# Past rows of the convolutions stored in one piece per partition, evictions of the in-projection ranked first, and 32x32 products alternating between two quadrants

## The chip, the cores and the metric

The kernel runs on one core of a Trainium2 chip. The metric is the device time of one execution in microseconds (us), from three runs. A profile of one further execution gives the spans and rows used below; its TensorE clock is told as the granted clock, 1.00 for 2.4 GHz and 0.50 for 1.2 GHz.

## The reference, cut to what matters

One inference step of a decoder trunk of two layers, all in float32, for a prompt of 512 tokens without a past and 8 samples of one token each with a past. Layer 0 mixes tokens by causal pooling, layer 1 by a gated delta rule over 8 heads of 128; each is followed by a ConvFFN. The three convolutions need the last rows of the past, and the new past rows are outputs.

```python
def conv_ffn(xn, buf, w_up, conv_w, conv_b, w_down):       # buf: last 2 up-projected rows
    hh = jnp.concatenate([buf, xn @ w_up], axis=1)
    c = causal_depthwise_conv(hh, conv_w, t) + conv_b      # width 3
    gate, val = jnp.split(c, 2, axis=-1)
    return (jax.nn.silu(gate) * val) @ w_down, hh[:, -2:]

def deltanet_mixer(xn, conv_buf, s0, w_in, conv_w, ...):   # conv_buf: last 3 rows
    qkv, z, a, bb = jnp.split(xn @ w_in, ...)              # 1024 -> 4096 + 16
    qkv_all = jnp.concatenate([conv_buf, qkv], axis=1)
    q, k, v = jnp.split(silu(causal_depthwise_conv(qkv_all, conv_w, t)), 3)   # width 4
    o, s_new = gated_delta_rule(l2_norm(q) * 128 ** -0.5, l2_norm(k), v, g, beta, s0)
    o = rms_norm(o, o_norm_w) * silu(z)
    return o @ w_out, qkv_all[:, -3:], s_new               # rows and state are outputs
```

The delta rule is computed in chunks: a unit lower triangular matrix per chunk and head is inverted, and a scan over the chunks carries a 128x128 state S.

## The kernel before

**Layout.** Everything lies with channels on the 128 partitions and the 520 columns (512 of the prompt, 8 of the samples) along the free axis, in two halves of 256 and 264 columns. A weight matrix comes in chunks of 128x1024 (`wr`), by DMA from the SP queue two chunks ahead; ACT casts each to the upper part `wh`, DVE subtracts to get the lower part `wl`, and each product is three TensorE matmuls (`ps<-xh,wl`, `ps<-xl,wh`, `ps<-xh,wh`).

**The delta layer.** Its in-projection has 32 tiles (`tile_`, from line 1619): two halves of 24 matmuls each, into a ring of three PSUM half-banks, so that a half can begin when the one three before it has been evicted. The task `t_post` (line 1559) evicts both halves on DVE (`hb<-ps,rstd`, two `hb` buffers), then does the convolution: one ACT and three DVE operations (`c<-hb,vec,c`), SiLU on ACT. Beside the tiles run, for each of four pairs of heads: `t_em` and `t_head` (decay factors `em`, which come back spread over the partitions by the DMA `em<-gdr`, and the matrix `U`), `t_leaf` and `levels` (inversion: `levels` at line 1285 joins blocks of 32 to 64 to 128 by small products; the tiles `p1` and `p2` take 32x32 products, both named `p` in the trace), `t_scan` (the chain over four chunks: `p_s` on PE, `rho` on DVE, `ut` on ACT, `S` on DVE), `t_norm` (output `ot`, transposed into `pt`, times the gate into `oz`), and `t_sample`, the single step of the eight samples for this pair (state loads `s<-in_ssm`, one for each head, products `p_q`, small DVE operations `s_...`, result `so`). `t_split` makes `oh` and `ol`, the two parts of the out-projection's input, for one head each.

**The end of the layer.** After the last in-projection tile, line 1667 on, SP stores the new past rows (`dnc_p`, `dnc_s`) and then loads the first two residual tiles `x<-xsp`. The out-projection starts on the heads that are ready (k = 0 to 5, for two of its eight output tiles), and goes on to the heads of the last pair when their `oh` and `ol` are there. Its eviction adds `x`.

**What sets the order.** The program is written out at build time. `Clock` models when each engine is free; `Background` (line 252) holds tasks sorted by a priority number (lower goes first). Between matmuls `step` lets the first task go on whose operands, engine and condition are ready in the model. `t_post` has priority 1, waits until the model sees DVE free (`"DVE"` as second part of its `yield`), and has `t_em` at 1, `t_scan` at 0.8, `t_head` at 0.6 and `t_leaf` at 0.5 beside or ahead of it; `t_sample` has 3.5.

**The FFN.** 44 tiles of two halves per layer in the up-projection. For each, the past rows enter the sample columns, and POOL copies the last rows of `hb` into the buffers of the outputs (`st<-hb`, 8 columns, and `fo<-hb`, 2 columns). One load at the start and two stores at the end of the up-projection move them.

All instructions carry line 152 in the trace, the helper that records them, so rows are told apart by tiles.

Of the kernel before, what the change touches and what calls it, by code (L numbers as in the profile page):

```python
# [14 lines left out]
T, B = 512, 8  # L15
NT = T + B
# [371 lines left out]
def _emit(tc, nc, clk, E, P, a, o):  # L388
    V, S, G, PE, SP = (E[k] for k in ("DVE", "ACT", "POOL", "PE", "SP"))
# [32 lines left out]
    bc = lambda v, shape, axis: v.unsqueeze(axis).broadcast_to(shape)  # L422
# [35 lines left out]
    bg = Background(clk)  # L458
# [138 lines left out]
    def ffn_buffers(p):  # L597
        return p.tile([128, NE, 3, B], F32, "st")

    fcw = lambda l, i: vec[:, V_FC + (l * 3 + i) * NE:V_FC + (l * 3 + i) * NE + NE]  # L600

    def ffn_load(l, buf):
        SP.dma_start(out=buf[:, :, 0:2, :], in_=a["ffn_buf"][l])

# [200 lines left out]
    def ffn(l, res, buf, mk, half0):  # L805
        rstd = res.rstd
        with scope(f"ff{l}") as fp:
            gh = fp.tile([128, KF, NT], F32R, "gh")
            gl = fp.tile([128, KF, NT], F32R, "gl")
            fo = fp.tile([128, NE, 2], F32, "fo")  # L810
            if buf is None:
                buf = ffn_buffers(fp)
                ffn_load(l, buf)
            st = buf
# [10 lines left out]
            for e in range(NE):  # L825
# [4 lines left out]
                hb = hbuf()  # L830
# [13 lines left out]
                for i in (1, 0):  # L844
                    V.scalar_tensor_tensor(
                        out=c[:, T:], in0=st[:, e, i, :], scalar=cw(i)[:, e:e + 1], in1=c[:, T:], op0=ALU.mult, op1=ALU.add
                    )
                G.tensor_copy(st[:, e, 2, :], hb[:, 3 + T:])
                G.tensor_copy(fo[:, e, :], hb[:, 1 + T:3 + T])
                if e % 2 == 0:  # L850
# [7 lines left out]
            finish(pend)  # L858
            SP.dma_start(out=o["ffn_p"][l], in_=fo)
            SP.dma_start(out=o["ffn_s"][l], in_=st[:, :, 1:3, :])  # L860
            nr = mk()
# [98 lines left out]
    def delta_in(res, dp, oz, oz1, r8):  # L960
# [19 lines left out]
        for v in vts:  # L980
            G.memset(v, 0.0)
        dst = dp.tile([128, 24, 3, B], F32, "dst")
        SP.dma_start(out=dst, in_=a["dn_buf"])
        dsb = dp.tile([128, 24, B], F32, "dsb")
        dtm = dp.tile([128, 24, B], F32, "dtm", tag="lx")
        cw = lambda i: vec[:, V_DC + i * 24:V_DC + i * 24 + 24]
        G.tensor_tensor(out=dsb, in0=dst[:, :, 0, :], in1=bc(cw(0), [128, 24, B], 2), op=ALU.mult)
        for i in (1, 2):
            G.tensor_tensor(out=dtm, in0=dst[:, :, i, :], in1=bc(cw(i), [128, 24, B], 2), op=ALU.mult)
            G.tensor_tensor(out=dsb, in0=dsb, in1=dtm, op=ALU.add)  # L990
# [298 lines left out]
        def levels(hh, vc, wc):  # L1289
# [14 lines left out]
            t0 = clk.at["PE"]  # L1304
            for i in (0, 2):
                s0, s1 = slice(32 * i, 32 * i + 32), slice(32 * i + 32, 32 * i + 64)
                for q in range(N2):
                    PE.matmul(p1[s1, q * 32:q * 32 + 32], u(q)[s0, s1], wc[s0, q, :], start=True, stop=True)
# [7 lines left out]
            p2 = aux("p2")  # L1316
            t0 = clk.at["PE"]
            s1 = slice(32, 64)
            for q in range(N2):
                PE.matmul(p2[s1, q * 32:q * 32 + 32], vc[s1, q, :], ysb[s1, q, :], start=True, stop=True)  # L1320
            for i in (0, 2):
                s0, s1 = slice(32 * i, 32 * i + 32), slice(32 * i + 32, 32 * i + 64)
                for q in range(N2):
                    PE.matmul(p2[s0, q * 32:q * 32 + 32], ysb[s1, q, :], vc[s1, q, :], start=True, stop=True)
            lite(t0)
# [232 lines left out]

        def t_post(i, n, halves, dst_ap, fin, pre):
            yield [halves[0], rstd[:]], "DVE", lambda: (i < 2 or i - 2 in read) and (i < 3 or i - 3 in posted)  # L1560
            hb = hbuf()
            for j in range(2):
                if j:
                    yield [lambda: clk.ready(halves[1]) + 0.1], "DVE", lambda: i in emitted
                V.tensor_tensor(out=hb[:, 3 + HS[j].start:3 + HS[j].stop], in0=halves[j], in1=rstd[:, HS[j]], op=ALU.mult)
                half_read.add((i, j))
            yield [hb[:]], "ACT", pre
            dst_ap = dst_ap() if callable(dst_ap) else dst_ap
# [46 lines left out]
        def tile_(n, dst_ap, fin, pre=None):  # L1615
            i = idx[0]
            idx[0] += 1
            bg.until(lambda: W.nl > W.nt and (i < 2 or (i - 2, 1) in half_read))
            ring = ((2 * i - 2) % 3, (2 * i - 1) % 3) if i else (2, 3)
            bg.settle(max([psd["p"].free_at(f"r{ring[0]}", 1)] + [clk.ready(w[:]) for w in W.peek()]) + 0.27)  # L1620
            halves = [dense_half(ring[0], 0), None]

            def mid():
                bg.add(t_post(i, n, halves, dst_ap, fin, pre), 1)
                bg.until(lambda: i < 1 or (i - 1, 0) in half_read)
                bg.settle(psd["p"].free_at(f"r{ring[1]}", 1) + 0.27)
# [39 lines left out]
        bg.until(lambda: n_in - 1 in posted and n_in - 2 in posted)  # L1666
        SP.dma_start(out=o["dnc_p"], in_=dnew[:, :, 0:3])
        SP.dma_start(out=o["dnc_s"][:, :, 0:2, :], in_=dst[:, :, 1:3, :])
        SP.dma_start(out=o["dnc_s"][:, :, 2, :], in_=dnew[:, :, 3:])
        for n, parts in (("oh", oh), ("ol", ol)):  # L1670
# [50 lines left out]
_OUT = {  # L1721
    "y": (128, KD, NT), "pool_p": (15, D), "pool_s": (128, KD, B, 15), "dnc_p": (128, 24, 3), "dnc_s": (128, 24, 3, B),
    "dns_p": (NH, 128, 128), "dns_s": (B, NH, 128, 128), "ffn_p": (2, 128, NE, 2), "ffn_s": (2, 128, NE, 2, B),
}


def _pack(i):
# [25 lines left out]
        "dn_out": c(tiles(i["dn_w_out"][0], KD).reshape(KD, 128, KD * 128)),  # L1753
        "ffn_buf": c(i["state_ffn_conv"].reshape(2, B, 2, NE, 128).transpose(0, 4, 3, 2, 1)[:, :, order]),
        "dn_buf": c(i["state_dn_conv"][0].reshape(B, 3, 24, 128).transpose(3, 2, 1, 0)),
        "ssm": c(i["state_dn_ssm"][0]),
# [34 lines left out]
```

## Time and profile before

| | |
|---|---|
| three runs | 1178.58, 1173.41, 1178.0 us; median 1178.0 |
| profiled execution | 1176.59 us, span 1174.9 us, mean granted clock 0.992 |
| PE | busy 1143.4 us, 97% of the span, 9576 matmuls |
| DVE | busy 793.5 us, 68% |
| ACT | busy 518.2 us, 44% |
| POOL | busy 404.6 us, 34% |
| chain that ended last | PE 87%, DVE 5%, DMA 3%, SP's queue 2% |

PE is the engine that is nearly always busy; what the others do matters where PE waits. In the table of stretches a stretch in which PE is busy 12.50 of 12.50 us has no wait to take away. A row of a timeline that ends in brackets tells how long the engine was idle before it and what ended that. The delta layer lies between about 425 and 755 us.

### The profile page before, as it was taken

To read this page: it belongs to the slowest core of one execution; us is meant where nothing else is said; L and a number is where in the kernel's file an instruction comes from. 1 tells how busy PE (TensorE), PEld (TensorE's weight loads), DVE (VectorE), ACT (ScalarE), POOL (GpSimd) and SP (SyncE) were. 2 spreads that over 40 slices of the span, in tenths; PEclk is the share of its full clock that TensorE was granted. 3 is DMA by queue.
4 is the path that set the end of the run, shared out by engine and by line. 5 is a ranking of instruction groups with operands and counts; after the bars stand their busy time and mean duration, and the time that the engine had idled before them with its cause. 6 is when DMAs were issued, how large, how long until landed. Compare 5 with 4: busy or idle time off the path is not lost.

```text
span 1174.9 us, 23548 instructions
## 1 busy us (share of the span) xinstructions
PE 1143.4 (97%) x9576; PEld 1120.8 (95%) x9576; DVE 793.5 (68%) x1464; ACT 518.2 (44%) x959; POOL 404.6 (34%) x610
## 2 busy tenths in 40 slices
PE   9999999999999999999899999799999999999996
PEld 8999999999999998999799998799999999999996
DVE  7877777777333377866778765469998989952224
ACT  5544444444322247765566734444444444432222
POOL 4233222222000011555463360225555555511011
PEclk9999999999999999999999999999999999999998
DMA  9222232323433233332233239535445444552322
GB/s 285 92 90 91 90 93 90 102 90 95 128 108 103 92 124 91 102 99 62 71 96 100 68 109 27 153 87 170 144 139 149 145 126 144 148 134 85 98 81 73
DMA packets 100974, 128.45 MB, mean 109 GB/s; under 512 B 37276, under 2 KB 72860, under 8 KB 100867
## 3 DMA queue, kind: packets, MB, share of 16 engines
q1 hardware_dynamic: 100723, 126.69, 38.8%
q8 instruction: 75, 1.23, 0.4%
q10 hardware_dynamic: 144, 0.26, 0.1%
q14 instruction: 32, 0.26, 0.1%
HBM read 116.20 MB, written 10.74 MB: 108 GB/s over the span
## 4 chain that ended last, share of the span: by engine, by line
PE 87%; DVE 5%; DMA 3%; SPq 2%; ACT 1%; issue 1%; DVEq 0%; POOL 0%; ACTq 0%; POOLq 0%
PE ps L152 78%; PE ps_d L152 2%; SPq L152 2%; DMA em<-gdr 1%; PE p L152 1%; PE p_s L152 1%; PE pk L152 1%; PE p_q L152 1%; DVE wl L152 1%; PE pt L152 1%; DVE em L152 1%; DVE c L152 1%; PE po L152 1%; DVE x L152 1%; DMA s<-in_ssm 1%
## 5 line engine op out<-in xcount | busy, mean ns | idle before, releaser
L152 PE MATMUL ps<-xh,wl 128*128 128x264 f32 (+1 forms) x1920 | 547.4, 285 | 6.1 <-DVE hb L152 6.1
L152 PE MATMUL ps<-xl,wh 128*128 128x256 f32 (+2 forms) x1936 | 550.5, 285 | 0.0
L152 PE MATMUL ps<-xh,wh 128*128 128x256 f32 (+2 forms) x1936 | 550.0, 284 | 0.0
L152 PEld LDWEIGHTS ps<-xh,wl 128*128 128x128 f32 x1920 | 362.4, 189 | 9.4 <-DVE hb L152 7.1
L152 PEld LDWEIGHTS ps<-xh,wh 128*128 128x128 f32 (+1 forms) x1936 | 364.1, 188 | 1.3 <-issue 0.8
L152 PEld LDWEIGHTS ps<-xl,wh 128*128 128x128 f32 (+1 forms) x1936 | 363.8, 188 | 1.5 <-issue 0.8
L152 DVE TENSOR_TENSOR wl<-wr,wh 128x1024 fp32r<-128x1024 f32 (+1 forms) x175 | 217.3, 1242 | 107.9 <-ACT wh L152 107.9
L152 ACT CAST wh<-wr 128x1024 fp32r<-128x1024 f32 (+1 forms) x177 | 180.4, 1020 | 215.8 <-PE ps L152 174.3
L152 DVE SCALAR_TENSOR_TENSOR c<-hb,vec,c 128x512 f32<-128x512 f32 x248 | 219.2, 884 | 11.1 <-ACT c L152 6.7
L152 POOL COPY st<-hb 128x8 f32<-128x8 f32 x88 | 73.0, 830 | 301.4 <-DVE hb L152 301.4
L152 PE MATMUL ps<-gl,wh 128*128 128x256 f32 (+1 forms) x616 | 174.5, 283 | 0.0
L152 PE MATMUL ps<-gh,wl 128*128 128x256 f32 (+1 forms) x616 | 174.0, 283 | 0.0
L152 PE MATMUL ps<-gh,wh 128*128 128x256 f32 (+1 forms) x616 | 173.8, 282 | 0.0
L152 DVE TENSOR_TENSOR hb<-ps,rstd 128x520 f32<-128x520 f32 (+2 forms) x152 | 87.5, 581 | 88.6 <-PE ps L152 87.9
L152 ACT ACTIVATE c<-hb,vec 128x520 f32<-128x520 f32 x112 | 89.9, 804 | 87.9 <-DVE hb L152 86.9
L152 POOL TENSOR_TENSOR acc<-acc,sq 128x520 f32<-128x520 f32 (+2 forms) x30 | 40.7, 1356 | 243.0 <-ACT sq L152 243.0
L152 PEld LDWEIGHTS ps<-gh,wh 128*128 128x128 f32 x616 | 116.3, 189 | 0.0
L152 PEld LDWEIGHTS ps<-gl,wh 128*128 128x128 f32 x616 | 115.9, 188 | 0.0
L152 PEld LDWEIGHTS ps<-gh,wl 128*128 128x128 f32 x616 | 115.7, 188 | 0.0
L152 ACT CAST gh<-c 128x520 fp32r<-128x520 f32 x44 | 27.6, 628 | 109.6 <-DVE c L152 109.6
L152 POOL COPY fo<-hb 128x2 f32<-128x2 f32 x88 | 74.2, 843 | 0.0
L152 ACT ACTIVATE sg<-c 128x520 f32<-128x520 f32 x44 | 28.1, 639 | 94.4 <-DVE c L152 94.4
(273 smaller groups left out, 1403.4 us busy)
## 6 DMA issues: line engine op xcount, KB each, us to landing
wr<-in_up SPq DMA_DIRECT2D x88, 512.0 KB, 3.5
wr<-in_dn_in SPq DMA_DIRECT2D x32, 512.0 KB, 3.5
wr<-in_down SPq DMA_DIRECT2D x32, 448.0 KB, 3.3
wr<-in_down SPq DMA_DIRECT2D x16, 512.0 KB, 3.5
s<-in_ssm SPq DMA_DIRECT2D x8, 512.0 KB, 4.1
wr<-in_dn_out SPq DMA_DIRECT2D x8, 512.0 KB, 3.5
s<-in_ssm SPq DMA_DIRECT2D x16, 256.0 KB, 4.0
s_ub<-udr SPq DMA_DIRECT2D x16, 256.0 KB, 4.4
```

The lines of the kernel that those rows point to most:

```text
L152: r = f(*a, **k)
```

## The change

Three edits, independent of each other.

1. The buffers of past rows are turned round, `[partition, channel tile, row, sample]` to `[partition, row, channel tile, sample]`, and the new row goes with the prompt's rows (`dnew`, `fo`), so that each load and store is one contiguous piece per partition; the outputs are put together on the host. For the FFN, one POOL copy of 10 columns takes the place of two of 8 and 2.
2. The eviction of an in-projection tile becomes a task of its own, `t_evict`, with priority -1, and no longer asks that the model see DVE free. `t_post` follows with the rest.
3. The 32x32 products of `p1` and two thirds of those of `p2` are issued alternately for two pairs of quadrants of the PE array; before, one quadrant's came after the other's.

```diff
-        return p.tile([128, NE, 3, B], F32, "st")
+        return p.tile([128, 2, NE, B], F32, "st")
-        SP.dma_start(out=buf[:, :, 0:2, :], in_=a["ffn_buf"][l])
+        SP.dma_start(out=buf, in_=a["ffn_buf"][l])
...
-                G.tensor_copy(st[:, e, 2, :], hb[:, 3 + T:])
-                G.tensor_copy(fo[:, e, :], hb[:, 1 + T:3 + T])
+                G.tensor_copy(fo[:, e, :], hb[:, 1 + T:])
...
-            SP.dma_start(out=o["ffn_p"][l], in_=fo)
-            SP.dma_start(out=o["ffn_s"][l], in_=st[:, :, 1:3, :])
+            SP.dma_start(out=o["ffn_n"][l], in_=fo)
+            SP.dma_start(out=o["ffn_o"][l], in_=st[:, 1])
...
-        dst = dp.tile([128, 24, 3, B], F32, "dst")
+        dst = dp.tile([128, 3, 24, B], F32, "dst")
...
-            for i in (0, 2):
-                s0, s1 = slice(32 * i, 32 * i + 32), slice(32 * i + 32, 32 * i + 64)
-                for q in range(N2):
+            for q in range(N2):
+                for i in (0, 2):
+                    s0, s1 = slice(32 * i, 32 * i + 32), slice(32 * i + 32, 32 * i + 64)
                     PE.matmul(p1[s1, q * 32:q * 32 + 32], u(q)[s0, s1], wc[s0, q, :], start=True, stop=True)
...
             for q in range(N2):
                 PE.matmul(p2[s1, q * 32:q * 32 + 32], vc[s1, q, :], ysb[s1, q, :], start=True, stop=True)
-            for i in (0, 2):
-                ...
-                    PE.matmul(p2[s0, q * 32:q * 32 + 32], ysb[s1, q, :], vc[s1, q, :], start=True, stop=True)
+                second(2, q)
+            for q in range(N2):
+                second(0, q)
...
-        def t_post(i, n, halves, dst_ap, fin, pre):
-            yield [halves[0], rstd[:]], "DVE", lambda: (i < 2 or i - 2 in read) and (i < 3 or i - 3 in posted)
+        def t_evict(i, n, halves, dst_ap, fin, pre):
+            yield [lambda: clk.ready(halves[0]) + 0.1, rstd[:]], None, lambda: (i < 2 or i - 2 in read) and (i < 3 or i - 3 in posted)
             hb = hbuf()
             for j in range(2):
                 if j:
-                    yield [lambda: clk.ready(halves[1]) + 0.1], "DVE", lambda: i in emitted
+                    yield [lambda: clk.ready(halves[1]) + 0.1], None, lambda: i in emitted
                 V.tensor_tensor(out=hb[:, 3 + HS[j].start:3 + HS[j].stop], in0=halves[j], in1=rstd[:, HS[j]], op=ALU.mult)
                 half_read.add((i, j))
+            bg.add(t_post(i, n, hb, dst_ap, fin, pre), 1)
...
-                bg.add(t_post(i, n, halves, dst_ap, fin, pre), 1)
+                bg.add(t_evict(i, n, halves, dst_ap, fin, pre), -1)
...
-        SP.dma_start(out=o["dnc_p"], in_=dnew[:, :, 0:3])
-        SP.dma_start(out=o["dnc_s"][:, :, 0:2, :], in_=dst[:, :, 1:3, :])
-        SP.dma_start(out=o["dnc_s"][:, :, 2, :], in_=dnew[:, :, 3:])
+        SP.dma_start(out=o["dnc_n"], in_=dnew)
+        SP.dma_start(out=o["dnc_o"], in_=dst[:, 1:3])
```

Since the planner writes the order out, the new priority moves instructions on every engine of the delta layer. On SP, around the end of the in-projection, before (`s` are state loads of the samples, `udr` and `dns_p` stores of results, `wr` weight chunks):

```order
103 L152 DMA s_8790<-in_ssm 128x8x128
104 L152 DMA wr<-in_dn_out 128x1024
105 L152 DMA s_8885<-in_ssm 128x8x128
106 L152 DMA udr<-s_ur 16x128
107 L152 DMA out_dnc_p<-dnew 3072x1x3
108 L152 DMA out_dnc_s<-dst 3072x1x16
109 L152 DMA out_dnc_s<-dnew 3072x1x8
110 L152 DMA x_9039<-xsp 128x520
111 L152 DMA x_9041<-xsp 128x520
112 L152 DMA wr<-in_dn_out 128x1024
113 L152 DMA out_dns_p<-S_9178 128x128
114 L152 DMA out_dns_p<-S_9188 128x128
```

And now:

```order
97 L152 DMA s_8707<-in_ssm 128x8x128
98 L152 DMA s_8799<-in_ssm 128x8x128
99 L152 DMA wr<-in_dn_out 128x1024
100 L152 DMA out_dnc_n<-dnew 128x264
101 L152 DMA out_dnc_o<-dst 128x384
102 L152 DMA x_8856<-xsp 128x520
103 L152 DMA x_8858<-xsp 128x520
104 L152 DMA udr<-s_ur 16x128
105 L152 DMA s_9022<-in_ssm 128x8x128
106 L152 DMA out_dns_p<-S_9055 128x128
107 L152 DMA s_9091<-in_ssm 128x8x128
108 L152 DMA out_dns_p<-S_9106 128x128
```

Both state loads of the last pair stood ahead of the stores of the past rows; now they stand behind the `x` loads, and the second also behind the store of a head's last `S`.

On DVE, around the second pair's decay factors, before (the first `em` of the piece waits for its DMA; `wl` is a weight chunk's lower part, `ot` the output of the first pair):

```order
558 L152 SCALAR_TENSOR_TENSOR oz<-pt,vec,oz 128x512
559 L152 TENSOR_TENSOR hb_88<-ps,rstd 128x264
560 L152 TENSOR_SCALAR epsq<-n_6670 128x4
561 L152 SCALAR_TENSOR_TENSOR em<-em,lg,msk 128x128
562 L152 TENSOR_TENSOR wl<-wr,wh 128x1024
563 L152 TENSOR_TENSOR ot_6367<-ot_6367,ms_6368 128x512
564 L152 SCALAR_TENSOR_TENSOR em<-em,lg,msk 128x128 x4
565 L152 TENSOR_SCALAR oz<-pt,vec 128x512
566 L152 SCALAR_TENSOR_TENSOR em<-em,lg,msk 128x128 x3
```

And now:

```order
564 L152 SCALAR_TENSOR_TENSOR oz<-pt,vec,oz 128x512
565 L152 TENSOR_TENSOR hb_88<-ps,rstd 128x264
566 L152 TENSOR_TENSOR ot_6308<-ot_6308,ms_6309 128x512
567 L152 TENSOR_SCALAR epsq<-n_6634 128x4
568 L152 SCALAR_TENSOR_TENSOR em<-em,lg,msk 128x128
569 L152 TENSOR_TENSOR wl<-wr,wh 128x1024
570 L152 TENSOR_SCALAR oz<-pt,vec 128x512
571 L152 TENSOR_TENSOR hb_89<-ps,rstd 128x256
572 L152 SCALAR_TENSOR_TENSOR em<-em,lg,msk 128x128 x7
573 L152 TENSOR_TENSOR hb_89<-ps,rstd 128x264
```

`ot` has moved ahead of the first `em`, and the next eviction `hb_89`, which stood eleven rows behind this piece, now stands in it.

On DVE, around the last eviction of the in-projection and the first chunk of the last pair's scan (`S<-p_s` by COPY), before: the `S` copies stand at 801 and 802, the last eviction, `hb_88<-ps,rstd 128x264`, at 819. Now:

```order
783 L152 TENSOR_TENSOR hb_88<-ps,rstd 128x264
784 L152 TENSOR_TENSOR wl<-wr,wh 128x1024
785 L152 TENSOR_TENSOR ol<-oz,oh 128x520 x2
786 L152 COPY S_8898<-p_s 128x128
787 L152 COPY S_8911<-p_s 128x128
788 L152 SCALAR_TENSOR_TENSOR rho_8924<-p_s,negc,vn 128x128
```

The whole scan of the last pair now stands behind the in-projection's last eviction.

And at the end of the layer, now (the last pair's sample step, and the first eviction of the out-projection):

```order
845 L152 COPY s_ur<-p_q 16x128
846 L152 TENSOR_SCALAR s_r<-p_q 16x1
847 L152 TENSOR_SCALAR s_d<-ident,s_r 16x16
848 L152 SCALAR_TENSOR_TENSOR so<-s_o,vec,p_q 128x16
849 L152 TENSOR_TENSOR oz<-so,oz 128x8 x2
850 L152 TENSOR_TENSOR ol<-oz,oh 128x520 x2
851 L152 TENSOR_TENSOR x_9204<-x_8856,ps 128x256
```

Before, this step (`s_ur` at 820, `oz<-so,oz` at 830) stood ahead of the scan's third chunk; now it is the last thing ahead of the last two `ol`.

## Rows read from the trace of the kernel before

**Rows 1.** Stretches: from:to, length, busy PE, PEld, DVE, ACT, POOL (instructions), clock, DMA share, GB/s

```profile
287.50:300.00 12.50, 12.50 (x107) 12.50 (x106) 7.10 (x10) 4.65 (x6) 1.64 (x2) 1.00 0.70 151
450.00:462.50 12.50, 10.67 (x70) 9.78 (x69) 10.56 (x25) 6.97 (x29) 2.87 (x6) 0.86 0.31 64
562.50:575.00 12.50, 10.18 (x67) 9.62 (x66) 10.28 (x23) 6.99 (x8) 4.28 (x13) 0.86 0.12 43
725.00:737.50 12.50, 10.78 (x86) 10.04 (x86) 6.26 (x13) 5.30 (x17) 1.99 (x2) 1.00 1.69 21
750.00:762.50 12.50, 11.71 (x86) 11.71 (x87) 7.38 (x13) 6.10 (x12) 5.25 (x5) 0.86 0.27 89
```

**Rows 2.** Waits of PE: waiting tile, releaser, us in total, times, longest

```profile
PE ps L152 <- DVE hb L152: 6.1, 4, 2.3
PE pt L152 <- DVE ot L152: 2.5, 1, 2.5
```

**Rows 3.** Timeline of SP's queue: start, us of issuing, what, count

```profile
704.66 0.38 SPq L152 DMA_DIRECT2D s<-in_ssm  x1
...
719.19 12.65 SPq L152 DMA_DIRECT2D out_dnc_s<-dnew  x1
731.88 5.76 SPq L152 DMA_DIRECT2D x<-xsp  x2
```

**Rows 4.** Timeline of PE where it waits: start, us, what, count, [idle before]

```profile
452.99 0.39 PE L152 MATMUL ps<-xh,wl 128*128 128x264 f32 x1 [1.83 <-DVE hb L152]
569.42 0.59 PE L152 MATMUL ps<-xh,wl 128*128 128x264 f32 x1 [2.32 <-DVE hb L152]
735.27 0.39 PE L152 MATMUL ps<-oh,wl 128*128 128x256 f32 x1 [0.93 <-ACT oh L152]
740.18 0.39 PE L152 MATMUL ps<-oh,wl 128*128 128x256 f32 x1 [1.52 <-DVE x L152]
744.95 0.39 PE L152 MATMUL ps<-oh,wl 128*128 128x264 f32 x1 [1.68 <-DVE x L152]
750.79 0.58 PE L152 MATMUL ps<-oh,wl 128*128 128x256 f32 x1 [2.63 <-DVE wl L152]
```

**Rows 5.** Timeline of DVE around the second pair's decay factors

```profile
558.05 0.40 DVE L152 SCALAR_TENSOR_TENSOR em<-em,lg,msk 128x128 f32<-128x128 f32 x1 [3.46 <-DMA em<-gdr]
558.37 1.21 DVE L152 TENSOR_TENSOR wl<-wr,wh 128x1024 fp32r<-128x1024 f32 x1
```

**Rows 6.** Timeline of PE, one `p1`, from its start to 521.79, 521.89 and 522.35

```profile
521.41 0.54 PE L152 MATMUL p<-lwc,U 32*32 32x32 f32 x12
521.41 0.67 PE L152 MATMUL p<-lwc,U 32*32 32x32 f32 x19
521.41 1.08 PE L152 MATMUL p<-lwc,U 32*32 32x32 f32 x32
```

**Rows 7.** Chain of waits, one `p2`: start, us, what

```profile
526.85 1.43 PE p L152 x48
```

**Rows 8.** Timeline of DVE, end of the delta layer

```profile
712.78 0.29 DVE L152 COPY S<-p_s 128x128 f32<-128x128 f32 x1 [4.84 <-PE p_s L152]
715.87 0.42 DVE L152 TENSOR_TENSOR hb<-ps,rstd 128x264 f32<-128x264 f32 x1
722.82 0.21 DVE L152 TENSOR_SCALAR s_d<-ident,s_r 16x16 f32<-16x16 f32 x1
724.07 0.24 DVE L152 TENSOR_TENSOR oz<-so,oz 128x8 f32<-128x8 f32 x2
727.69 0.35 DVE L152 SCALAR_TENSOR_TENSOR S<-S,eg,p_s 128x128 f32<-128x128 f32 x1 [1.19 <-PE p_s L152]
```

**Rows 9.** The sample step: a row of POOL's timeline, and DMAs (KB, us to landing)

```profile
716.73 0.54 POOL L152 TENSOR_TENSOR s_r<-s_r,half 16x1 f32<-16x1 f32 x1 [13.81 <-DVE s_r L152]
...
s<-in_ssm SPq DMA_DIRECT2D x8, 512.0 KB, 4.1
```

**Rows 10.** Costliest groups of the page, POOL: busy, mean ns | idle before

```profile
L152 POOL COPY st<-hb 128x8 f32<-128x8 f32 x88 | 73.0, 830 | 301.4 <-DVE hb L152 301.4
```

More of the change, by code (lines that the diff above doesn't have):

```diff
@@ L809, in ffn @@
             gl = fp.tile([128, KF, NT], F32R, "gl")
-            fo = fp.tile([128, NE, 2], F32, "fo")
+            fo = fp.tile([128, NE, 2 + B], F32, "fo")
             if buf is None:
@@ L845, in ffn @@
                     V.scalar_tensor_tensor(
-                        out=c[:, T:], in0=st[:, e, i, :], scalar=cw(i)[:, e:e + 1], in1=c[:, T:], op0=ALU.mult, op1=ALU.add
+                        out=c[:, T:], in0=st[:, i, e, :], scalar=cw(i)[:, e:e + 1], in1=c[:, T:], op0=ALU.mult, op1=ALU.add
                     )
-                G.tensor_copy(st[:, e, 2, :], hb[:, 3 + T:])
-                G.tensor_copy(fo[:, e, :], hb[:, 1 + T:3 + T])
+                G.tensor_copy(fo[:, e, :], hb[:, 1 + T:])
                 if e % 2 == 0:
@@ L986, in delta_in @@
         cw = lambda i: vec[:, V_DC + i * 24:V_DC + i * 24 + 24]
-        G.tensor_tensor(out=dsb, in0=dst[:, :, 0, :], in1=bc(cw(0), [128, 24, B], 2), op=ALU.mult)
+        G.tensor_tensor(out=dsb, in0=dst[:, 0], in1=bc(cw(0), [128, 24, B], 2), op=ALU.mult)
         for i in (1, 2):
-            G.tensor_tensor(out=dtm, in0=dst[:, :, i, :], in1=bc(cw(i), [128, 24, B], 2), op=ALU.mult)
+            G.tensor_tensor(out=dtm, in0=dst[:, i], in1=bc(cw(i), [128, 24, B], 2), op=ALU.mult)
             G.tensor_tensor(out=dsb, in0=dsb, in1=dtm, op=ALU.add)
@@ L1317, in levels, with second @@
             t0 = clk.at["PE"]
+            def second(i, q):
+                s0, s1 = slice(32 * i, 32 * i + 32), slice(32 * i + 32, 32 * i + 64)
+                PE.matmul(p2[s0, q * 32:q * 32 + 32], ysb[s1, q, :], vc[s1, q, :], start=True, stop=True)
             s1 = slice(32, 64)
@@ L1320, in levels @@
                 PE.matmul(p2[s1, q * 32:q * 32 + 32], vc[s1, q, :], ysb[s1, q, :], start=True, stop=True)
-            for i in (0, 2):
-                s0, s1 = slice(32 * i, 32 * i + 32), slice(32 * i + 32, 32 * i + 64)
-                for q in range(N2):
-                    PE.matmul(p2[s0, q * 32:q * 32 + 32], ysb[s1, q, :], vc[s1, q, :], start=True, stop=True)
+                second(2, q)
+            for q in range(N2):
+                second(0, q)
             lite(t0)
@@ L1563, in t_post @@
                 if j:
-                    yield [lambda: clk.ready(halves[1]) + 0.1], "DVE", lambda: i in emitted
+                    yield [lambda: clk.ready(halves[1]) + 0.1], None, lambda: i in emitted
                 V.tensor_tensor(out=hb[:, 3 + HS[j].start:3 + HS[j].stop], in0=halves[j], in1=rstd[:, HS[j]], op=ALU.mult)
                 half_read.add((i, j))
+            bg.add(t_post(i, n, hb, dst_ap, fin, pre), 1)
+        def t_post(i, n, hb, dst_ap, fin, pre):
             yield [hb[:]], "ACT", pre
@@ L1721 @@
 _OUT = {
-    "y": (128, KD, NT), "pool_p": (15, D), "pool_s": (128, KD, B, 15), "dnc_p": (128, 24, 3), "dnc_s": (128, 24, 3, B),
-    "dns_p": (NH, 128, 128), "dns_s": (B, NH, 128, 128), "ffn_p": (2, 128, NE, 2), "ffn_s": (2, 128, NE, 2, B),
+    "y": (128, KD, NT), "pool_p": (15, D), "pool_s": (128, KD, B, 15), "dnc_n": (128, 24, 3 + B), "dnc_o": (128, 2, 24, B),
+    "dns_p": (NH, 128, 128), "dns_s": (B, NH, 128, 128), "ffn_n": (2, 128, NE, 2 + B), "ffn_o": (2, 128, NE, B),
 }
@@ L1753, in _pack @@
         "dn_out": c(tiles(i["dn_w_out"][0], KD).reshape(KD, 128, KD * 128)),
-        "ffn_buf": c(i["state_ffn_conv"].reshape(2, B, 2, NE, 128).transpose(0, 4, 3, 2, 1)[:, :, order]),
-        "dn_buf": c(i["state_dn_conv"][0].reshape(B, 3, 24, 128).transpose(3, 2, 1, 0)),
+        "ffn_buf": c(i["state_ffn_conv"].reshape(2, B, 2, NE, 128).transpose(0, 4, 2, 3, 1)[:, :, :, order]),
+        "dn_buf": c(i["state_dn_conv"][0].reshape(B, 3, 24, 128).transpose(3, 1, 2, 0)),
         "ssm": c(i["state_dn_ssm"][0]),
@@ L1765, in _unpack @@
     y = r["y"].transpose(2, 1, 0).reshape(NT, D)
+    dnc_s = np.concatenate([r["dnc_o"], r["dnc_n"][:, None, :, 3:]], 1)
+    ffn_s = np.stack([r["ffn_o"], r["ffn_n"][..., 2:]], 2)
     return (
@@ L1769, in _unpack @@
         c(r["pool_s"].transpose(2, 3, 1, 0).reshape(1, B, 15, D)),
-        c(r["dnc_p"].transpose(2, 1, 0).reshape(1, 1, 3, 3072)),
-        c(r["dnc_s"].transpose(3, 2, 1, 0).reshape(1, B, 3, 3072)),
+        c(r["dnc_n"][:, :, :3].transpose(2, 1, 0).reshape(1, 1, 3, 3072)),
+        c(dnc_s.transpose(3, 1, 2, 0).reshape(1, B, 3, 3072)),
         c(r["dns_p"][None, None]), c(r["dns_s"][None]),
-        c(r["ffn_p"][:, :, inv].transpose(0, 3, 2, 1).reshape(2, 1, 2, 2 * FF)),
-        c(r["ffn_s"][:, :, inv].transpose(0, 4, 3, 2, 1).reshape(2, B, 2, 2 * FF)),
+        c(r["ffn_n"][:, :, inv, :2].transpose(0, 3, 2, 1).reshape(2, 1, 2, 2 * FF)),
+        c(ffn_s[:, :, :, inv].transpose(0, 4, 2, 3, 1).reshape(2, B, 2, 2 * FF)),
     )
```

## The prediction

> **What bounds the kernel now.** I began with the table of stretches [rows 1]. In the FFN, as in 287.5 to 300, PE is busy 12.50 of 12.50 us at a clock of 1.00: nothing that another engine does there can come back as time. Only the delta layer, 425 to 755 us, has gaps, and three of its stretches (450, 562.5 and 750) show a clock of 0.86, so part of each was run at the lower level, 1.2 GHz. At 0.86 for 12.5 us, 0.14 x 12.5 = 1.75 us of full-speed work is lost, each time beside a wait of PE of 1.8 to 2.6 us.
>
> Next came the list of PE's waits [rows 2]: evictions (`hb`) 6.1 us in four places, `ot` 2.5 us in one. The timeline places them [rows 4]: 1.83 us before 452.99 and 2.32 us before 569.42 on `hb`, then at the end of the layer 1.52, 1.68 and 2.63 us on `x` and `wl`. I then followed these last three back. Two belong to evictions of the out-projection, the third to its weights, whose load stands behind the `x` loads in the order. The queue of SP [rows 3] shows why these were late: the store `out_dnc_s<-dnew` occupied the queue for 12.65 us from 719.19, the two `x` loads for another 5.76 from 731.88. The stretch from 725 to 737.5 shows a DMA share of 1.69 while only 21 GB/s were moved [rows 1]: the DMA engines had much to do with few bytes. The order names the reason: the store is `3072x1x8`, pieces of 32 bytes.
>
> **The change part by part.** The sum is made against the profiled execution, 1176.6 us, which is 1.4 us below the median of the three runs, 1178.0.
>
> *Stores of `dnc`.* Now `128x264` and `128x384`, so 256 pieces of over 1 KB instead of thousands; the `x` loads and a weight chunk follow at once. The waits 1.52 + 1.68 + 2.63 = 5.83 us [rows 4] and the lower clock behind them, 1.75 us [rows 1], may go: -7.6. What is late next is the heads' own input: PE waited 0.93 us for `oh` at 735.27 [rows 4], ahead of these. If a similar chain of `x` and weights remains, only about 3 is won; that is the weak end.
>
> *FFN loads, stores and copies.* 88 POOL copies of 830 ns [rows 10] go, and POOL had been idle 301 us in front of them; the loads and stores lie beside a PE that is full [rows 1]. 0. Without that cover one store at a layer's end could cost a few us, but neither stretch around it shows a gap. Bounds -1 to +1.
>
> *Evictions first.* The order shows how the wait at 569.42 comes: DVE stood 3.46 us at `em` for its DMA, behind it `wl` (1.21), `ot` and the rest of `em` [rows 5], convolutions, and only then the next eviction. Now `ot` stands ahead of `em` and `hb_89` four rows behind it. At most it gives all `hb` waits (6.1), `ot` (2.5) [rows 2] and two spells of lower clock (3.5): 12.1. At least I count 2, if DVE, busy 10.3 and 10.6 of 12.5 us in these stretches [rows 1], only makes PE wait for something else. I take the two long waits and their clock, 1.83 + 2.32 + 3.5 = 7.7, and leave the short ones and `ot` uncounted: -7.7. The price is that convolutions, `em` and the scan come behind evictions; that is counted below.
>
> *32x32 products.* A `p1` has begun 12 products after 0.38 us and 32 after about 1.00, some 32 ns each; but from the twelfth to the nineteenth, where the second quadrant's begin, seven took 0.10 us, 14 ns each [rows 6]. So two quadrants can run side by side. If all of `p1` goes at about 16 ns, 1.00 falls to 0.51; in a `p2` of 48 on the path for 1.43 [rows 7] the 32 alternating ones fall likewise. That is 1.0 us per pair, less some 0.3 for three junctions that overlapped already: 0.7 x 4 pairs = -2.8. Bounds 0 and -4.
>
> Here a rule speaks against it. All products of one `p1` write one tile of PSUM, and the Trainium skill (TensorEngine Tiling (Array Packing), Restrictions and Gotchas, Gotcha 1: PSUM Pressure) says that different row tiles can't access the same PSUM bank at the same time. By the rule this term is 0; the seven products in 0.10 us speak against the rule, at least for disjoint partitions.
>
> *The scan's place.* Before, the last pair's first `S` copy began at 712.78, 3.1 us ahead of the last eviction at 715.87 [rows 8]. Now it stands behind that eviction (0.42), a `wl` (1.21, [rows 5]) and two `ol`, of which I take the `wl`'s length for both together: at most 3.1 + 0.4 + 1.2 + 1.2 = 5.9 us later against the end of the in-projection. PE has only the out-projection on k = 0 to 5 for filling, and had little to spare, since it waited at 735.27 already. None of it counts if DVE has time to spare there, so 0 to 5.9: I take the middle, +3.
>
> *The samples' place.* Before, the last pair's sample step ended at 724.07 + 0.24, 11 us before `oh` was missed, hidden. Now its second state load is issued behind the store of a head's last `S`, which ended at 727.69 + 0.35 = 728.0 [rows 8]. The load takes 4.1 [rows 9]. Before, the same load was issued at 704.66 [rows 3], so it was there at 708.8, and from there to `oz` at 724.3 the step took 15.5 us. Of these, `s_d` spent 5.5 behind other work on DVE (POOL's `s_r` ended at 717.27, `s_d` began at 722.82 [rows 8, 9]), and I estimate that another 3 went by beside the scan's and evictions' rows. That leaves 7: 728.0 + 4.1 + 7 = 739.1, some 4 us behind 735.27. +4, bounds 0 (the last head's output comes later anyway) and 8 (with the lower clock after the wait, and the casts).
>
> Sum: 1176.6 - 7.6 - 7.7 - 2.8 + 3 + 4 = 1165.5, said as 1166.
>
> **The rivals.**
>
> *The wait is only renamed (B).* DVE is at 82 to 85% in the two stretches [rows 1] and `em` still waits for its DMA; evictions first delay convolutions and `U`, and PE waits for them. Then evictions give 2, not 7.7: 1171.2. For it: the order puts two evictions beside the `em` without taking any DVE work away. Against: PE's list names `hb` and `ot` alone in this place.
>
> *No overlap in the PE array (C).* The two streams go into one tile of PSUM and take turns there: the 2.8 falls away, 1168.3. Against it are the seven products in 0.10 us where two streams meet [rows 6]; for it, that these are one junction's and not a whole product's. The Trainium skill's rule above would give this time.
>
> *The stores were not what made `x` late (E).* If the tiles that `x` goes into, or SP's place behind other things, set the time of the load, its 7.6 stays: 1173.1. Against: the queue's rows are back to back from 719.19 to 737.64 [rows 3], and PE's first wait on `x` ends right behind.
>
> *The samples take the tail over (D), slower.* The place is SP's queue at the end of the layer, and the mechanism that the step keeps its old pace: from the second load's issue at 704.66 to `oz` at 724.31 it took 19.7 us [rows 3, 8]. From 728.0 that ends at 747.7, 12.4 us behind 735.27; one spell of lower clock adds 1.75, the scan's place 5.9. This cost of 20 us stands against 7.6 from the stores and, since evictions and products only shorten what comes before the tail's chain, 2 from these: 1176.6 + 10.4 = 1187. It decides from the point where scan and samples together cost over 18.1, what the forecast wins elsewhere. For it: the step passes through SP, PE, ACT, DVE and POOL one after the other and has nothing beside it then. Against: with little else left, what it queued behind, over half of those 15.5 us, is gone too.
>
> **How the numbers follow.** Forecast 0.56, B 0.19, C 0.08, E 0.09, D 0.08. Half a per cent, 5.9 us, is about what a measurement of this kernel can tell from no change: faster is below 1172.1, slower above 1183.9. Faster: 0.54 + 0.12 + 0.07 + 0.03 = 0.76; same: 0.02 + 0.07 + 0.01 + 0.06 + 0.01 = 0.17; slower 0.07. The range: with every gain at its strong end and the tail at no cost 1176.6 - 7.6 - 12.1 - 4 = 1152.9, with gains at the weak end (3, 2, 0) and the tail at its middle 1178.6. Neither end has all its parts at once: 1155 to 1176, which holds B, C and E.
>
> **What would show it.** In the profile after: SP's issue of the two `dnc` stores under 2 us each and the `x` loads landed before PE needs them; no wait of PE on `hb` above 1 us and a clock of 1.00 around the second pair's `em`; a `p1` of some 0.6 us; PE waiting for `oh` or `ol` of the last heads once, 3 to 8 us, at the end of the layer. Wrong would be: an `x` still late, PE's list with a new name of 3 us or more before the tail, or a wait for the samples above 10 us.

## The result and the profile after

The changed kernel took 1159.7 us in the median of four runs (1157.5 to 1160.9), the one before 1176.6. The quotient of these medians is 0.9856; the ratio on record is 0.9843, with an interval of 0.9816 to 0.9871 that holds both. A second series gave 0.9847 (0.9828 to 0.9866). The forecast was 1166, its range 1155 to 1176. So the direction and the range held, and the gain was half as large again as the sum made it: 17 us by these medians, 18 by the ratios, in place of 11.

The profiled span went from 1174.9 to 1156.9 us. First the list of what PE waited for, in the changed kernel (waiting tile, releaser, us in total, times, longest), against [rows 2]:

```profile
PE ps L152 <- ACT oh L152: 1.6, 2, 1.2
PE p_q L152 <- DVE s_d L152: 1.5, 1, 1.5
...
PE p_q L152 <- DVE s_u L152: 0.7, 1, 0.7
...
PE p_q L152 <- DVE s_t L152: 0.7, 1, 0.7
```

`hb` (6.1 us) and `ot` (2.5) are gone from it altogether, and so are the waits on `x` and `wl` at the end of the layer (5.83 us [rows 4]). What is new are the waits of `p_q` on `s_d`, `s_u` and `s_t`, the last pair's sample step; `oh` had been waited for before, for 0.93 us [rows 4]. The stretches, in the columns of [rows 1], say the same by place:

```profile
287.50:300.00 12.50, 12.50 (x106) 12.50 (x106) 7.12 (x11) 5.55 (x6) 0.99 (x1) 1.00 0.52 151
450.00:462.50 12.50, 12.50 (x97) 12.18 (x96) 10.14 (x24) 7.87 (x31) 1.95 (x5) 1.00 0.37 119
525.00:537.50 12.50, 12.50 (x100) 12.07 (x101) 7.26 (x29) 5.73 (x22) 7.08 (x26) 0.86 0.03 10
562.50:575.00 12.50, 12.50 (x170) 12.14 (x170) 10.55 (x23) 9.17 (x30) 6.53 (x13) 1.00 0.23 61
712.50:725.00 12.50, 8.30 (x56) 6.72 (x55) 6.59 (x26) 3.02 (x4) 1.41 (x2) 0.74 0.38 127
725.00:737.50 12.50, 12.50 (x92) 12.50 (x92) 7.82 (x15) 7.76 (x15) 3.72 (x4) 0.85 0.19 66
```

At 450 and 562.5 PE is now full at a clock of 1.00, where it had been busy 10.67 and 10.18 us at 0.86 [rows 1]. The FFN is as full as it was. The gap has moved to 712.5 to 725. SP's queue there, in the columns of [rows 3]:

```profile
694.35 0.38 SPq L152 DMA_DIRECT2D out_dnc_n<-dnew  x1
694.79 0.42 SPq L152 DMA_DIRECT2D out_dnc_o<-dst  x1
695.26 1.04 SPq L152 DMA_DIRECT2D x<-xsp  x2
701.70 0.32 SPq L152 DMA_DIRECT2D udr<-s_ur  x1
702.13 0.38 SPq L152 DMA_DIRECT2D s<-in_ssm  x1
707.45 0.34 SPq L152 DMA_DIRECT2D out_dns_p<-S  x1
709.76 0.38 SPq L152 DMA_DIRECT2D s<-in_ssm  x1
```

Two stores occupy the queue for 0.38 and 0.42 us instead of 12.65 for one of them, and the `x` loads follow at once. The second state load, at 709.76, is what the end of the layer now waits for. What held it was not the store at 707.45. SP stood another 2.3 us, which its list of waits puts down to PE, until the products of the pair's first head had ended (709.06 + 0.64 = 709.70). Both heads' states go into one buffer (`s0` in `t_sample`), so the second can't be loaded before the first has been read. PE's timeline shows the products of the two heads and, behind them, the step as four waits one after the other (0.74 + 0.65 + 1.48 + 1.18 = 4.05 us):

```profile
709.06 0.64 PE L152 MATMUL p_q<-s,ksm 128*32 128x256 f32 x8
...
713.80 0.64 PE L152 MATMUL p_q<-s,ksm 128*32 128x256 f32 x8
...
718.20 0.27 PE L152 MATMUL p_q<-ident,s_u 128*16 128x128 f32 x1 [0.74 <-DVE s_u L152]
719.12 0.21 PE L152 MATMUL p_q<-ones,s_t 128*16 128x1 f32 x2 [0.65 <-DVE s_t L152]
720.81 0.58 PE L152 MATMUL p_q<-s_d,ones 16*128 16x16 f32 x2 [1.48 <-DVE s_d L152]
722.56 0.58 PE L152 MATMUL ps<-oh,wl 128*128 128x256 f32 x1 [1.18 <-ACT oh L152]
```

The same products of `p1` that had taken 1.08 us from 521.41 [rows 6] now read, in the timeline around the first pair:

```profile
514.10 0.69 PE L152 MATMUL p<-lwc,U 32*32 32x32 f32 x32
```

And a `p2`, in the chain of waits (which counts 47 of its 48 rows), against 1.43 us [rows 7]:

```profile
635.48 1.03 PE p L152 x47
```

The kernel issues 16 matmuls for a `p1` and 24 for a `p2`; the trace shows each of them as two rows. What the prediction prices as one product (32 ns, 16 ns) is therefore one row, half a matmul. Its sums in us don't depend on this.

### The profile page after: what moved, and what is told of

Same layout as the page of the kernel before. It is cut to its first block, busy times and chain, and to the rows that moved or that the text cites. A ratio compares the mean times of both kernels' runs of the same rounds, so it can differ in the third digit from the quotient of the medians.

```text
span 1156.9 us, 23466 instructions
## 1 busy us (share of the span) xinstructions
PE 1137.3 (98%) x9576; PEld 1116.5 (97%) x9576; DVE 791.1 (68%) x1464; ACT 519.1 (45%) x959; POOL 350.4 (30%) x522
## 3 DMA queue, kind: packets, MB, share of 16 engines
q8 instruction: 75, 1.23, 0.4%
## 4 chain that ended last, share of the span: by engine, by line
PE 93%; DVE 2%; ACT 2%; DMA 1%; issue 1%; DVEq 0%; POOL 0%; POOLq 0%; ACTq 0%
PE ps L152 83%; PE ps_d L152 2%; PE p_s L152 2%; PE pt L152 1%; PE p_q L152 1%; PE po L152 1%; PE p L152 1%; PE pk L152 1%; DMA s<-in_ssm 1%; DVE x L152 1%; ACT jk L152 0%; DVE xl L152 0%; DMA xt<-in_xt 0%; PE ps_n L152 0%; DVE c L152 0%
## 5 line engine op out<-in xcount | busy, mean ns | idle before, releaser
L152 DVE TENSOR_TENSOR wl<-wr,wh 128x1024 fp32r<-128x1024 f32 (+1 forms) x175 | 223.0, 1274 | 106.2 <-ACT wh L152 106.1
L152 DVE SCALAR_TENSOR_TENSOR c<-hb,vec,c 128x512 f32<-128x512 f32 x248 | 210.2, 848 | 7.2 <-ACT c L152 3.0
L152 POOL COPY fo<-hb 128x10 f32<-128x10 f32 x88 | 72.3, 821 | 357.1 <-DVE hb L152 357.1
L152 POOL TENSOR_TENSOR lx<-lx,lt 128x60 f32<-128x60 f32 (+24 forms) x124 | 54.4, 439 | 9.7
```

The source lines that it names most:

```text
L152: r = f(*a, **k)
```

## The experiments

First each edit alone, and the changed kernel with one taken out, so that what each is worth beside the others can be read. Ratios are to the kernel before, in the same series of runs. The first three rows come from one series, the next two from a second and the last from a third, each on another chip.

| kernel | ratio | interval | median, us |
|---|---|---|---|
| layout alone | 0.9944 | 0.9915 to 0.9972 | 1172.9 |
| alternating products alone | 0.9964 | 0.9945 to 0.9983 | 1174.4 |
| evictions first alone | 0.9974 | 0.9954 to 0.9994 | 1175.3 |
| all but evictions first | 0.9896 | 0.9877 to 0.9915 | 1167.8 |
| all but alternating products | 0.9851 | 0.9827 to 0.9876 | 1162.3 |
| all three | 0.9847 | 0.9828 to 0.9866 | 1159.8 |

**Layout alone.** The kernel before with the first edit:

```diff
-        dst = dp.tile([128, 24, 3, B], F32, "dst")
+        dst = dp.tile([128, 3, 24, B], F32, "dst")
-        SP.dma_start(out=o["dnc_s"][:, :, 2, :], in_=dnew[:, :, 3:])
+        SP.dma_start(out=o["dnc_n"], in_=dnew)
...
```

> The kernel before with the new layout of the past rows alone (loads, stores, one POOL copy). Theory: the whole gain lies at the end of the delta layer, where the store of 12.65 us held up the x loads: the waits on x and wl (1.52 + 1.68 + 2.63) and the lower clock behind them (1.75) go, 7.6 us, 1169.0; in the trace the FFN of layer 0 and 1 last as long as before (383.1 us from the first up-projection of layer 1 to the end). Rival E: x is late for another reason, 1176.6. A second rival: what is next in line, oh of the last heads, takes over half of it, 1173.

It gained 0.56%, 6.6 us. PE's waits on `x` and `wl` are gone from its list, and the `oh` wait (0.9) is all that is left there, as in [rows 4]. The last matmul of the program lies 383.1 us behind the first up-projection matmul of layer 1 in this kernel, in the one before and in the changed one, and layer 0's FFN lasts 382.1 us before and 381.8 in the other two: the FFN part is worth nothing. But its eleven runs fall into two groups, three at 1166.4 to 1167.4 and eight at 1172.3 to 1175.1. The profiled one, at 1172.9, points to the reason:

```profile
700.00:712.50 12.50, 12.50 (x119) 10.31 (x118) 2.50 (x10) 2.27 (x5) 0.55 (x1) 0.55 0.27 85
712.50:725.00 12.50, 12.10 (x91) 11.15 (x87) 6.33 (x27) 7.33 (x24) 0.54 (x1) 0.91 0.22 71
```

For most of the first stretch PE ran at 1.2 GHz while fully busy; (0.45 + 0.09) x 12.5 = 6.8 us were lost, about the distance of the two groups. Its mean granted clock was 0.993 and 0.994 in the three quick runs and 0.985 to 0.989 in the others. Against the four runs of the kernel before with a clock of 0.992, its best in this series (1173.45 to 1175.46 us), the quick three lie 7.5 us lower, so the size of the gain holds at a nearly equal clock.

**Alternating products alone.**

```diff
-            for i in (0, 2):
+            for q in range(N2):
-                for q in range(N2):
+                for i in (0, 2):
...
```

> The kernel before with the alternating 32x32 products alone. Theory: p1 goes from 1.02 to 0.62 us and p2 from 1.43 to 1.03 in each of four pairs, as in the changed kernel, and since PE is full around three of the four, about 3.2 us come off: 1173.4. Rival: the time won falls into PE's waits on DVE in the same layer, 1176.

0.36%, 4.2 us with an interval of 2 to 6.5. From the start of the first product to the next matmul of another tile, `p1` fell from 1.02 to 0.62 us and `p2` from 1.43 to 1.03 in every pair of the changed kernel: 0.8 x 4 = 3.2.

**Evictions first alone.**

```diff
+        def t_evict(i, n, halves, dst_ap, fin, pre):
...
-                bg.add(t_post(i, n, halves, dst_ap, fin, pre), 1)
+                bg.add(t_evict(i, n, halves, dst_ap, fin, pre), -1)
```

> The kernel before with the evictions ranked first alone. Two theories. The edits add up: the changed kernel's 17 us less the 7.6 of the stores and 3.2 of the products, 1170.4. They don't, since the samples' step of the last pair now stands behind the stores on SP's queue: its first state load, 702.1 in the changed kernel, comes some 18 us later (14.8 us of stores and 5.8 of x loads in place of 1.8), the step takes as long as there, so the wait of PE for the last heads grows by 12 us and more, with the lower clock: 1175 to 1182. In the in-projection itself no wait on hb above 1 us in either case.

The second theory held: 1175.3 us, a gain of only 0.26%. No wait on `hb` is left in the list, but at the end of the layer one new row of PE's timeline eats most of what this gave. The four waits of the sample step, 4.05 us, and stretches at a clock of 0.63, 0.91 and 0.78 from 712.5 to 750 follow it:

```profile
722.15 1.08 PE L152 MATMUL p_q<-s,ksm 128*32 128x256 f32 x8 [10.77 <-DMA s<-in_ssm]
```

Its SP queue names the reason; the state load stands behind the same long store:

```profile
700.14 13.44 SPq L152 DMA_DIRECT2D out_dnc_s<-dnew  x1
713.62 3.33 SPq L152 DMA_DIRECT2D x<-xsp  x2
717.00 0.43 SPq L152 DMA_DIRECT2D udr<-s_ur  x1
717.53 0.39 SPq L152 DMA_DIRECT2D s<-in_ssm  x1
```

**The changed kernel with the evictions as before.**

```diff
-                bg.add(t_evict(i, n, halves, dst_ap, fin, pre), -1)
+                bg.add(t_post(i, n, halves, dst_ap, fin, pre), 1)
...
```

> The changed kernel with the evictions as before (layout and alternating products stay). If the eviction edit was worth 3 us, as it was alone, 1163. If the edits don't add up, because alone the samples' step paid for it behind the long stores, the layout's 0.56% and the products' 0.36% remain, 1167 to 1168, and the eviction edit is worth some 8 us here; in the trace the waits on hb at about 453, 480, 569 and 619 (2.0, 1.3, 2.5, 1.3) and on ot at 560 are back.

1167.8 us, 0.9896. What the edit had taken away is back in PE's list:

```profile
PE ps L152 <- DVE hb L152: 6.8, 4, 2.3
PE pt L152 <- DVE ot L152: 1.8, 1, 1.8
```

Beside the other two, the evictions are worth 0.49%, some 6 us (3 to 9 by the intervals), and alone 0.26%; beside the layout alone 0.93% (0.9944 to 0.9851). The layout is worth 0.56% alone and 1.23% beside the evictions (0.9974 to 0.9851). By the times alone it isn't certain that the edits fail to add up: what the evictions gain in company is 0.67%, give or take 0.43, in the second comparison, into which the slow stretch of the kernel with the layout alone enters, and 0.23%, give or take 0.33, in the first. The mechanism is in the traces: the layout takes away the long store behind which the new order puts the state load, and with it the wait of 10.77 us. That the evictions in turn take away something that spoils the layout isn't shown.

**The changed kernel with the products one after the other.** The edit is the reverse of that of the products alone.

> The changed kernel with the 32x32 products one quadrant after the other, as before. Theory: p1 and p2 take 0.8 us more in each of four pairs, 1163. Rival: the lower clock from 527.4 to 530.9 in the changed kernel comes from the alternating products and goes with them, 1.7 us: 1161.

0.9851 against 0.9847, with intervals of 0.005 and 0.004: this pair can't tell 3.2 us from nothing. The run that was profiled had a spell of lower clock elsewhere (0.50 from 687.5 to 700). The stretch at 525 stands at 1.00 in it, as the rival wants; but so it does in the second profile of the changed kernel, which has the alternating products, so the rival isn't shown either.

**The samples' place.** The theory for the gap that is left at the end of the layer is the samples' low rank. Five variants of the changed kernel tried to close it. One number for all pairs:

```diff
-            bg.add(t_sample(pair), 3.5)
+            bg.add(t_sample(pair), 0.9)
```

> The changed kernel with one number changed: the samples' task has priority 0.9 in place of 3.5, so that the order puts the last pair's state loads ahead of the stores and x loads, and its step beside the scan. Theory: the 4.6 us that PE waits for the last pair's samples at 718 to 724 and the lower clock from 718.6 to 728.8 (half of 10.2 us, 5.1) go: 1150. Weaker: the samples' steps push other chains back and only half comes, 1155. Rival: the end of the scan sets the tail and the samples only fill it, 1159.7.

0.9877 (0.9847 to 0.9907): slower than the changed kernel, against all three of the expectations. The intervals overlap, but all six runs (1161.8 to 1167.0) lie above all nine of the changed kernel, taken on other chips. The waits for samples are gone from the end, but PE waits there for `ot` (1.5) and `oh` (1.1), and earlier 2.6 us for state loads, 1.7 of them at 523; and it ran at the lower clock for part of five stretches:

```profile
525.00:537.50 12.50, 12.50 (x91) 11.45 (x91) 6.67 (x26) 7.13 (x23) 2.06 (x3) 0.73 0.01 3
587.50:600.00 12.50, 12.17 (x104) 11.20 (x104) 8.69 (x31) 9.43 (x27) 5.08 (x18) 0.86 0.15 46
687.50:700.00 12.50, 11.96 (x161) 10.46 (x160) 5.55 (x20) 4.02 (x8) 2.43 (x8) 0.88 0.39 122
700.00:712.50 12.50, 12.50 (x86) 10.93 (x86) 6.57 (x23) 7.02 (x17) 0.00 (x0) 0.71 0.44 137
725.00:737.50 12.50, 9.51 (x63) 8.92 (x62) 7.07 (x14) 7.42 (x13) 2.20 (x3) 0.86 0.37 132
```

With (0.27 + 0.14 + 0.12 + 0.29 + 0.14) x 12.5 = 12 us at stake, this is 5 more than in the changed kernel's three slow stretches (0.14 + 0.26 + 0.15, 6.9 us), and its span is 5.8 us longer.

The same for the last pair alone (`0.9 if pair == 3 else 3.5`):

> The changed kernel with priority 0.9 for the samples' task of the last pair alone (3.5 for the others). With 0.9 for all pairs the profile had four spells of lower clock in the delta layer (526, 594, 697, 731), 23.9 us in all, 12 us lost, where the changed kernel has two, 13.7 us, 6.8 lost: 5 us, which is the whole difference of the two. Theory: the spells come where small products crowd, and pairs 0 to 2 in their old place bring none; the last pair's step is out of the tail: 1155. Rival: the last pair's crowding is enough, a spell of 10 us or so at about 697 stays: 1160 to 1165.

0.9859 (0.9840 to 0.9878), no gain. Its PE still waits 1.97, 1.08 and 1.18 us on that step: the last pair's task can't begin until the third's is done, and that one kept its low rank. A theory about the wrong pair. The spell at 697 that the rival expected isn't there either (1.00 from 687.5 to 712.5).

For the third and fourth pair (`0.9 if pair >= 2 else 3.5`):

> The changed kernel with priority 0.9 for the samples' task of the third and fourth pair. Both state loads of the last pair stand ahead of the stores. Theory: the samples' waits at the end go (4.6 us) without the lower clock that 0.9 for all pairs brought at 526 and 594 (5.1 us): 0.980. Rival: PE's clock falls elsewhere or the scan's end sets the tail (with 0.9 for all pairs PE still waited 3.6 us for ot and oh of the last heads): 0.984 or more.

0.9813 (0.9794 to 0.9833), 1155.9 us (1155.6 to 1157.7) against 1159.8 (1157.3 to 1161.1) of the changed kernel on the same chip. The intervals overlap slightly, but three of its four runs are below all five of the other's. It is the quickest version tried, though not clear of the changed kernel. Its list has what the theory asked for: the 3 us on `p_q` for `s_d`, `s_u` and `s_t` are gone, and `oh` is the largest wait of that place (of the rows below, the first lies at 524 and the last at 619).

```profile
PE p_q L152 <- DMA s<-in_ssm: 1.3, 1, 1.3
PE ps L152 <- ACT oh L152: 1.1, 1, 1.1
...
PE ps L152 <- DVE hb L152: 0.8, 1, 0.8
```

With priority 2 for all pairs, and with 0.55:

> The changed kernel with priority 2 for the samples' task of all pairs. The order puts the last pair's first state load ahead of the stores, the second still behind the scan's end. Theory of the tail (it ends with this second load, 4.1 us, and the chain behind it of 8.7 us): the same waits of about 4.6 us and no gain, 0.984 of before. Rival: an earlier start of the step is enough, 0.980.

> The changed kernel with priority 0.55 for the samples' task of all pairs, ahead of t_head and t_scan. Both state loads of the last pair stand ahead of the stores, the step's last products beside the scan's first chunk. Theory: as with 0.9, the waits for samples go and others and lower clock come, 0.986 to 0.988; if the crowding of small products is less than with 0.9, 0.981.

0.9896 and 0.9884, both slower than the changed kernel. With 2 the waits for the step stay (1.21, 0.66, 1.48 and 1.18 us in the timeline), and two waits of 1.52 and 2.46 us on `ot` come back, earlier in the layer. So both expectations for 2 were too good; for 0.55 the first was about right.

**Filling the waits.** Matmuls of 128x128 that nobody reads, 16 in all, in the places where PE waits for the last pair's samples; the last figure of `fill` is how many:

```diff
             p = aux("p_q")
+            fill(pair, p, 3)
             PE.transpose(p[:16, 0:128], flat(u_), ident)
+            fill(pair, p, 2)
...
```

> The changed kernel with 16 more matmuls of 128x128 whose results nobody reads, put on PE where it waits for the last pair's samples (3 before the transpose of s_u, 2 before the sum of s_t, 6 before the product with s_d and 5 behind it); all else stands in the same order. Theory: the lower clock from 718.6 to 728.8 comes from PE standing idle 4 us there; with the filling it stays at 1.00, and 5.1 us come back: 1155. Rival: the small products of 8 to 16 columns bring it down, or the filling delays what waits: 1159.7 or more.

0.9841 (0.9823 to 0.9859): nothing won. The clock did as the theory said in the first of these stretches, which stand at 0.74 and 0.85 in the changed kernel, and not in the second:

```profile
712.50:725.00 12.50, 11.63 (x94) 9.96 (x92) 5.66 (x26) 1.18 (x5) 1.55 (x2) 1.00 0.33 96
725.00:737.50 12.50, 11.53 (x79) 11.14 (x80) 7.65 (x14) 8.32 (x16) 2.24 (x3) 0.86 0.30 103
```

The spell came later, from 727.4 to 731.0, and lasted 3.6 us instead of 10.2. And the 5.1 us were mis-sized: of the slow time from 718.6 to 728.8, the part up to 722.6 was mostly spent waiting, where a slow clock costs nothing, so that some 3 us were to be had, of which the new spell cost 1.75 again. The step itself became longer, 7.7 us from the products with `s_x` to the first product of `oh` (717.88 to 725.62) in place of 6.6 (715.93 to 722.56): part of the filling stood in the way of what had been waited for.

**The changed kernel once more**, in the series of the last three variants:

> The changed kernel once more, as the measure for the three variants on the same chip: 0.9843 of before; its time and that of before should rise and fall with the mean granted clock, about 1.2 us for 0.001.

0.9847. In its profile the slow stretch at 525 is not there (1.00), in the same program; its span was 1155.1.

## Why the prediction was right, step by step

*Stores of `dnc`, -7.6: right, but for the clock in it.* Alone they gave 6.6 (interval 3.3 to 10). The waits named went, and what was late next was `oh`, as said. The rival E falls. The 1.75 us of lower clock don't go with these waits. In the kernel with the alternating products alone PE waits for `wl` as long as in [rows 4], and the stretch behind stands at 1.00 in place of 0.86 [rows 1]:

```profile
749.31 0.39 PE L152 MATMUL ps<-oh,wl 128*128 128x256 f32 x1 [2.63 <-DVE wl L152]
```

```profile
750.00:762.50 12.50, 12.50 (x107) 12.50 (x106) 7.01 (x13) 6.64 (x15) 5.87 (x5) 1.00 0.41 127
```

*FFN, 0: right*, by the 383.1 us of layer 1 in all three kernels and the 382.1 and 381.8 of layer 0.

*Evictions first, -7.7: the mechanism right, the term too small.* All `hb` waits went, not the two long ones alone, `ot` with them, and neither slow stretch is in the changed kernel: the 12.1 that had been put down as the upper bound. The 1.75 us of the stretch at 562.5 in it are doubtful, since this stretch stands at 1.00 also with the layout alone and in the changed kernel with the evictions as before, each with its `hb` wait of 2.3 to 2.4 us. A new slow stretch, at 525, takes 1.75 of it back in one profile and nothing in the other. The reason to hold back was rival B, that DVE at 82 to 85% would hand the wait on; there is no such wait in the list, so B falls in this place. The order had shown it: `ot` ahead of the `em` that waits, and the next eviction three rows behind that `em`. With all that they cost at the end of the layer, the evictions stood in the sum at -7.7 + 3 + 4 = -0.7; taking them out of the changed kernel cost 0.49%, some 6 us.

*32x32 products, -2.8: right.* 0.8 us per pair by the trace, 3.2 in all, where 0.7 per pair was forecast; `p1` came to 0.62, not 0.51. The time of the edit alone agrees (2 to 6.5 us); beside the other two edits the runs can't tell it from nothing. Rival C falls: the two streams don't simply take turns. The rule in the Trainium skill (TensorEngine Tiling (Array Packing), Restrictions and Gotchas, Gotcha 1: PSUM Pressure) is that different row tiles can't access the same PSUM bank at the same time. The 0.62 us in place of 1.02 speak against reading it, as the prediction did, as no gain at all. Whether the writes of the two quadrants, which go to separate partitions of the tile, ever fall together is not shown.

*The scan's place, +3, and the samples', +4.* The scan cost PE nothing of its own: in the changed kernel's list no wait on the scan's products is above 0.4 us. The samples cost more than 4: four waits of 4.05 us and about 3 us of slow clock behind them. The sum of both, +7, is what was found, from the second term alone; that is luck. The load's place, behind the store of a head's last `S`, was as forecast, but it wasn't what held the load: that was the buffer, in which the prediction saw no wait, 2.3 us beyond the store's issue. Whether a second buffer would have helped wasn't tried. The chain behind the load took 8.1 us (from 713.8, when its first products ran, to the end of `oz` at 721.9) where 7 were estimated. Rival D, in which the step keeps its pace of 19.7 us, didn't come: from the load's issue at 709.76 to the end of `oz` it took 12.2 us. It had little to queue behind; `s_d` began 0.02 us after POOL's `s_r` had ended, in place of 5.55 [rows 8, 9]. The 10.77 us in the run with evictions alone are of D's size, but come from the stores ahead of the load and not from the step's pace.

With the measured terms, -6.6 - 12.1 + 1.75 - 3.2 + 7 = -13 stand against 17 to 18. Some 4 us are not assigned to a step. Read from the runs instead, layout and products together gave 1.04% (12 us, where 10.4 had been forecast) and the evictions the other 0.49% (6 us, where 0.7 had been): most of the surplus lies in the evictions, as far as intervals of 2 to 3 us let one say. Part of it may be the interplay, in that the layout's gain is larger where the samples' loads would stand behind the stores; these were counted only against the old order. The prediction made two errors of method. It treated its terms as independent, and it read a lower clock in one profile as part of the price of the wait beside it. That the sum still erred to the safe side is luck: nothing in it said which way it would err.

## What to carry to other kernels

Two edits on one path have to be priced together: a better order here was worth 0.26% while a 13 us store stood in the queue behind which it put a load, and 0.49 to 0.93% once that store was short. The trace shows the wait that made the difference; the times alone would leave it open. Read each queue of the new order for what now stands behind its longest row, and for each load there, which buffer it has to wait for. Before a lower clock is priced with a wait, look whether another profile shows the one without the other. A task that is always last in rank ends up alone at the end of a phase, where nothing hides it; raise it where it starves and not everywhere (here from the third pair on, which looked best but isn't clear of the noise).

## What the runs showed of the hardware that was not expected

A store of 96 KB in pieces of 32 bytes occupied the queue of its issuing engine for 12.65 to 13.5 us in three kernels, and the one of 192 KB ahead of it, in pieces of 64 bytes, for 1.6 to 2.9; as one piece per partition 132 and 192 KB took some 0.4 us each in most of eleven profiles, 1.2 at most.

The trace shows each of the kernel's 16 small f32 matmuls of a `p1` as two rows, 32 ns apart where one quadrant follows the other (1.02 us for 32) and 19 ns where two quadrants alternate (0.62 us).

PE's clock fell to the lower level without a wait ahead of it. In the kernel with the layout alone it did so at about 701.4 and rose again at 714.2, with PE full in every stretch from 662.5 to 712.5; the stretch at 0.55 has 119 rows of matmuls in which small products (`p`, `p_q`) are mixed with full ones. In the changed kernel with the products one after the other, the stretch from 687.5 to 700 ran at 0.50 with PE full in it and in the four before. Such a spell comes in some runs of a program and not in others: the stretch at 525 of the changed kernel stands at 0.86 in one profile and at 1.00 in the other. With the layout alone the three quick runs and the other eight lie 7.0 us apart in the mean, at mean clocks of 0.994 and 0.987, so about 1.1 us for 0.001. What sets it off is not settled here: filling PE's waits shortened a spell, but spells also came where PE was busy, and waits of 2.3 to 2.6 us stood in some profiles with a spell behind them and in others without.
